# One decoder block on one core: a planner that charges changes of partitions, score products on quarters of the array, and a norm weight made from a column

## The chip, the core and the metric

The kernel runs on one core of one Trainium2 chip. The metric is device time in microseconds (us) of one execution. A core has a matrix engine (PE, with its weight loads shown as PEld), a vector engine (DVE), a scalar engine (ACT), GpSimd (POOL), and SyncE (SP), from which all loads and stores of this kernel are issued to 16 DMA engines. PE writes to PSUM, eight banks of 128 partitions by 512 f32 values; DVE and ACT read it from there.

## What is computed

One decoder block over 512 tokens of width 1024. Two groups of heads run side by side: RWKV-7 (eight heads of 64, a recurrence over tokens) and sparse attention with three branches; then an output projection and a SwiGLU feed-forward part.

```python
y = rmsnorm(h, norm1_w) @ w_in                       # one projection for both groups
# RWKV-7, for each token t and head:
sa = einsum('bhij,bhj->bhi', S, -kk_t)
S  = S * w_t + sa[..., None] * (kk_t * a_t) + v_t[..., None] * k_t
o_t = einsum('bhij,bhj->bhi', S, r_t)
# attention: softmax(q k / 8) v over compressed, selected and window keys, gated and added
h = h + concat([o_rwkv, o_nsa]) @ w_out
h = h + (silu(n2(h) @ ffn_w1) * (n2(h) @ ffn_w3)) @ ffn_w2
out = rmsnorm(h, final_norm_w)
```

## The kernel before

The kernel is written as a list of operations in program order (class Kern), which a planner (class Program) sorts. `add` records each operation and `cost` gives it a duration in ns. `layout` links it to those that it must wait for, and `schedule` walks through time: at each step the engine that is free first takes the ready operation of the highest rank. A rank is the longest path to the end, plus `ahead`, a priority that `go(part)` sets from the table PRIO. The planner also picks DVE or ACT for a copy (`nc.copy`), and a PSUM bank for each product. Each engine then executes its list in that order, fixed when the kernel is built. SP's queue is ordered in the same way.

For PE the planner keeps the array shape of each operation (`mode`: rows and columns, 32, 64 or 128). A change of shape costs 100 ns (L497 and L498), and an operation of the last shape is preferred if its rank is at most STAY below the best (L457). Matmuls that use other columns of the array than the one before are glued to it (`glue`, L260 to L265): they are placed together and count 53 or 27 ns. Two generators are woven together: `merge` runs the recurrences as the main stream and takes work from `filler` (projections, compression, attention) by RATIO; `zip` runs one pair's recurrence with the next pair's preparation, by ZIP.

The stages by the profile's clock: first norm and the first projection (0 to 20 us), further projections and the preparation of the first of four head pairs (to about 100), recurrences of the four pairs beside the projections (to about 300), attention (about 265 to 359), the output projection (to 402), the feed-forward part (to 740).

What the change touches:

- `consts` and `norm1` (first norm). The weight of the norm is loaded as a row and broadcast by the DMA to all 128 partitions (`n1w`, 512 KB), second in SP's order. `norm_T` squares a tile of x, takes the reciprocal root, multiplies by the weight on DVE, and transposes on PE.
- `rw_prep` prepares one pair of heads (p = 0 to 3, two heads on 64 partitions each). BKB holds for head 0 the columns [kk | k2] and for head 1 [k2 | kk], written by four multiplications on 64 partitions. For each head and each half of the chunks (cg) four matmuls of 64 rows by 128 columns fill one PSUM bank with scores, and one DVE multiplication by a mask moves the bank to SC. Then comes the substitution (`subst`: 45 short DVE operations, then 32x32 products from L1245 on, `doubl`), and later transposes of BK, eight for each head, to one bank a head.
- `attention`. A unit is a pair of query heads and a branch (eight units). `probs` computes and normalises the weights P. For each block j of 128 keys, the blocks of P of both heads are transposed on PE and copied out of PSUM (PT), and two 128x64 matmuls with v add to the bank `po`; then the next j.

Of the kernel before, what the change touches and what calls it, by code (L numbers as in the profile page):

```python
# [176 lines left out]
class Op:  # L177
    __slots__ = ("i", "eng", "name", "args", "kw", "r", "w", "dur", "pred", "succ", "banks", "rank", "n", "est", "start", "tag", "alt", "cols", "glue", "ahead", "beside", "mode", "work")
# [10 lines left out]
class Program:  # L189
# [7 lines left out]
    def __init__(self, tc):  # L197
        self.tc, self.nc = tc, tc.nc
        self.ops, self.slots, self.free, self.regions = [], [], {}, {}
        self.table, self.pre, self.side = [], None, None  # L200
        self.ahead = 0
        for e in self.ENG:
            setattr(self, e, Proxy(self.add, e))
# [24 lines left out]
    def add(self, eng, name, args, kw):  # L228
# [16 lines left out]
        op.dur = self.cost(op)  # L245
        if name == "preload_act_table_set":
# [6 lines left out]
        if eng == "tensor":  # L253

            m, c0 = size(kw["lhsT"]) if name == "matmul" else 128, op.w[0].p0 // 32
# [3 lines left out]
            p = 2 if name == "transpose" else 1 if kw["rhs"].dtype == R32 else 4  # L259
            op.work = p * size(op.w[0]) * l.n * size(l) / 128 ** 2  # L260
            op.cols = set(range(c0, c0 + m // 32))
            if self.side and not op.cols & self.side:
                self.ops[-1].glue = op
                self.side = self.side | op.cols
# [19 lines left out]
    def cost(self, op):  # L284
# [26 lines left out]
    STAY = 3000  # L311

    def moved(self, op):

        return math.prod((op.w + op.r)[0].shape) * 4 / 360
# [75 lines left out]
    def schedule(self):  # L391
# [33 lines left out]
        order, last_pe = [], None  # L425
        while len(order) < len(self.ops):
# [17 lines left out]
            while ready[e] and not op:  # L444
# [4 lines left out]
                if o.alt:  # L449
# [5 lines left out]
                    op = o  # L455
                    break
                if pick and pick[0][0] + self.STAY < x[0]:  # L457
# [7 lines left out]
                if not new or have >= self.RESERVE[new[0].key] + len(new):  # L465
                    same = e != "tensor" or not last_pe or o.mode == last_pe.mode
# [26 lines left out]
            if e == "sync" and len(out) == 8:  # L493
                t = max(t, out.pop(0))
            if e == "tensor":

                if last_pe and last_pe.mode != op.mode:  # L497
                    t += 100  # L498
# [12 lines left out]
            if e == "sync":  # L511
                dma = max(t + 1100, dma) + self.moved(op)
                end = dma + 900
# [62 lines left out]
class Kern:  # L576
# [150 lines left out]
    def consts(self):  # L727
        nc, a = self.nc, self.a
        self.cc = Split([(0, self.tl(self.cst, [128, 256], "cc")), (256, None)])
# [1218 lines left out]
```

## Time and profile before

| what | us |
|---|---|
| median of 3 runs (746.73 to 747.71) | 746.78 |
| the profiled execution | 746.66 |
| its span, first to last instruction | 744.8 |
| PE busy | 713.2 |
| DVE busy | 620.0 |
| ACT busy | 429.9 |

A line of the trace is L560 for nearly all instructions, since one loop issues them; rows are told apart by engine, operation and shape. A shape such as `64*128 64x128` is of a matmul on 64 rows and 128 columns of the array (rows*columns) that streams 128 values through each of the 64 rows. An ordinary f32 matmul is recorded as two instructions, a transpose or an fp32r matmul as one. Busy time is the union of the recorded intervals; ends of matmuls are modelled and run past the start of the next one.

### The profile page before, as it was taken

The page shows a single profiled execution, that of the slowest core. Times are in us where ns is not written, and L with a number is a line of the kernel's source. Part 1 is how long each engine was busy: PE and PEld are TensorE (multiplying, and loading weights), DVE is VectorE, ACT ScalarE, POOL GpSimd, SP SyncE. Part 2 cuts the span into 40 slices and gives each one's busy share as a digit, 9 for nine tenths or more (in the row PEclk, how much of TensorE's full clock was granted, in tenths as well). Part 3 has the DMA queues.
Part 4 walks back from the last instruction along what each step waited for, and adds up shares of the span by engine and source line. Part 5 has one row for each costly group of instructions (what it writes and reads, how often), then busy time and mean ns, then how long its engine had stood idle before and what let it go on. Part 6 is the DMA issues. An engine that isn't in the chain of part 4 may idle for free. (4 is left out here: it accounts for less than half of the span.)

```text
span 744.8 us, 14644 instructions
## 1 busy us (share of the span) xinstructions
PE 713.2 (96%) x5540; PEld 606.7 (81%) x5540; DVE 620.0 (83%) x1480; ACT 429.9 (58%) x948; POOL 3.7 (1%) x39
## 2 busy tenths in 40 slices
PE   5999999999989989999999999999999999999996
PEld 4988975768768666666788999999999999888785
DVE  6956988986997999798538999999999994687886
ACT  6555466554554688898336566565555552533545
POOL 0000000000000000000000000000000000000000
PEclk9999999999999999999999999999999999999999
DMA  8222326202110010533311233333333307464453
GB/s 318 72 77 62 98 78 199 75 27 74 41 31 28 16 45 1 170 103 96 114 57 71 72 114 114 114 120 108 114 100 114 101 22 258 159 216 149 139 171 116
DMA packets 39829, 77.37 MB, mean 104 GB/s; under 512 B 4432, under 2 KB 8912, under 8 KB 39760
## 3 DMA queue, kind: packets, MB, share of 16 engines
q1 hardware_dynamic: 39760, 76.45, 31.5%
q8 instruction: 43, 0.70, 0.4%
q14 instruction: 26, 0.21, 0.1%
HBM read 72.24 MB, written 4.19 MB: 103 GB/s over the span
## 5 line engine op out<-in xcount | busy, mean ns | idle before, releaser
L560 PE MATMUL ps<-s,s 128*128 128x256 f32 (+11 forms) x5412 | 710.4, 304 | 25.2 <-DVE s L560 19.1
L560 PEld LDWEIGHTS ps<-s,s 128*128 128x128 f32 (+5 forms) x5412 | 604.0, 170 | 130.2 <-DVE s L560 37.9
L560 DVE TENSOR_TENSOR s<-s,s 128x512 fp32r<-128x512 f32 (+18 forms) x662 | 378.4, 607 | 38.0 <-ACT s L560 18.9
L560 ACT ACTIVATE s<-s 128x512 fp32r<-128x512 f32 (+9 forms) x395 | 237.3, 619 | 226.7 <-DVE s L560 87.0
L560 ACT ACTIVATE s<-ps 128x256 f32<-128x256 f32 (+9 forms) x286 | 103.4, 376 | 43.2 <-PE ps L560 39.7
L560 DVE TENSOR_TENSOR s<-ps,s 128x256 f32<-128x256 f32 (+5 forms) x174 | 86.2, 506 | 29.7 <-PE ps L560 28.5
L560 ACT ACTIVATE s<-s,s 128x512 f32<-128x512 f32 (+4 forms) x142 | 72.1, 526 | 26.3 <-DVE s L560 25.0
L560 DVE COPY s<-ps 128x256 f32<-128x256 f32 (+6 forms) x77 | 32.4, 429 | 6.7 <-PE ps L560 5.4
L560 DVE CUSTOM_DVE_ANT_0 s<-ps,s 128x384 f32<-128x384 f32 (+3 forms) x64 | 29.8, 484 | 3.9 <-PE ps L560 3.7
L560 DVE SCALAR_TENSOR_TENSOR s<-s,s,s 128x512 f32<-128x512 f32 (+2 forms) x32 | 19.4, 630 | 13.8 <-DMA s<-in_n1w 6.6
L560 ACT ACTIVATE s<-ps,s 128x512 f32<-128x512 f32 (+1 forms) x34 | 20.1, 621 | 12.8 <-PE ps L560 12.6
L560 DVE SCALAR_TENSOR_TENSOR s<-ps,s,s 64x64 f32<-64x64 f32 (+1 forms) x62 | 23.9, 385 | 4.1 <-PE ps L560 1.5
L560 DVE CAST s<-s 128x512 fp32r<-128x512 f32 (+6 forms) x27 | 10.9, 409 | 14.5 <-PE ps L560 10.4
L560 DVE TENSOR_SCALAR s<-s,s 128x128 f32<-128x128 f32 (+4 forms) x67 | 21.4, 353 | 1.4 <-ACT s L560 0.8
L560 DVE STREAM_SHUFFLE s<-s 128x8 f32<-128x8 f32 (+14 forms) x60 | 14.0, 234 | 0.1
L560 ACT ACTIVATION_READ_ACCUMULATOR s<-s,s 128x1 f32 x64 | 12.1, 190 | 0.0
L560 DVE SCALAR_TENSOR_TENSOR s<-s,s 128x128 f32<-128x128 f32 (+1 forms) x26 | 8.9, 347 | 0.4
L560 ACT ACT_TABLE_LOAD x6 | 7.7, 1283 | 0.8 <-PEq L1935 0.7
L560 DVE TENSOR_TENSOR_SCAN s<-s,s 128x512 f32<-128x512 f32 x4 | 4.9, 1219 | 1.9 <-ACT s L560 1.9
L560 DVE COPY s<-s 64x512 f32<-64x512 f32 (+3 forms) x16 | 5.2, 323 | 0.8 <-PE ps L560 0.5
L560 DVE CAST s<-ps 128x512 fp32r<-128x512 f32 x7 | 4.8, 682 | 0.6 <-PE ps L560 0.6
L560 DVE DVE_READ_ACCUMULATOR2_ANT s<- 128x1 f32 x64 | 5.2, 82 | 0.0
(19 smaller groups left out, 41.2 us busy)
## 6 DMA issues: line engine op xcount, KB each, us to landing
s<-in_ffn_w SPq DMA_DIRECT2D x90, 256.0 KB, 2.7
s<-in_ffn_w SPq DMA_DIRECT2D x34, 512.0 KB, 3.8
s<-in_w_in_r SPq DMA_DIRECT2D x28, 256.0 KB, 2.7
s<-in_x SPq DMA_DIRECT2D x8, 512.0 KB, 5.4
s<-in_cw SPq DMA_DIRECT2D x16, 256.0 KB, 3.3
s<-in_w_out SPq DMA_DIRECT2D x8, 512.0 KB, 3.5
s<-in_w_in_n SPq DMA_DIRECT2D x8, 256.0 KB, 2.7
scr<-s SPq DMA_DIRECT2D x4, 512.0 KB, 2.6
```

The source lines that it names most:

```text
L560: ins = f(*[real(x) for x in op.args], **{k: real(x) for k, x in op.kw.items()})
```

## The change

- Planner: the array cells that a matmul uses are now pairs of row and column strips. A matmul is glued to those before it if it shares no cell with them, and no column strip in the same bank. DVE and ACT operations get a mode too, first partition and number of partitions, and a change is charged 110 ns. `keep` glues consecutive PE operations without condition. Latencies and DMA costs are changed (TOPE 80 instead of 120 towards PE, 80 more after f32 products, 300 instead of 360 bytes per ns), the scan costs 1140.
- Parameters: STAY is 500 for PE and 0 for the others; RATIO, ZIP and several priorities change.
- `rw_prep`: BKB is [kk | k2] for both heads, by two multiplications on 128 partitions. Each score matmul becomes two of 64x64, one for each output half; the four of a chunk lie on the four quarters of the array. The transposes of BK become products with the identity, in the same arrangement.
- `attention`: all transposes of a unit come first, then its eight matmuls with v, glued.
- `norm1`: the weight arrives as eight columns behind the first 256 columns of constants. Each half is copied to 128 columns a block by broadcast, transposed on PE, and copied out of PSUM.

```diff
@@ add
+        op.mode = (op.w[0].p0, op.w[0].n) if eng in ("vector", "scalar") and op.w else None
...
-            op.cols = set(range(c0, c0 + m // 32))
-            if self.side and not op.cols & self.side:
+            op.slow = p == 4
+            op.cols = {(r, c) for r in range(l.p0 // 32, l.p0 // 32 + op.mode[0] // 32) for c in range(c0, c0 + m // 32)}
+            bank, at = op.w[0].buf, {c for _, c in op.cols}
+            if self.side and not any(op.cols & q or at & {c for _, c in q} and b is bank for q, b in self.side):
                 self.ops[-1].glue = op
...
             else:
-                self.side = op.cols
+                if self.keep and self.ops and self.ops[-1].eng == "tensor":
+                    self.ops[-1].glue = op
+                self.side = [(op.cols, bank)]
@@ cost, lat, schedule
+        if op.name == "tensor_tensor_scan":
+            return 1140
...
-    STAY = 3000
+    TOPE = 80
+    STAY2 = 0
+    DRAIN = {"tensor": 100, "vector": 110, "scalar": 110, "gpsimd": 0, "sync": 0}
+    STAY = 500
...
-            t = self.LAT[p.eng] + (120 if op.eng == "tensor" else 0)
+            t = self.LAT[p.eng] + (self.TOPE if op.eng == "tensor" else 80 if p.eng == "tensor" and p.slow else 0)
...
-                if pick and pick[0][0] + self.STAY < x[0]:
+                if pick and pick[0][0] + (self.STAY if e == "tensor" else self.STAY2) < x[0]:
...
-                    same = e != "tensor" or not last_pe or o.mode == last_pe.mode
+                    same = last[e] in (None, o.mode)
...
+            if last[e] not in (None, op.mode):
+                t += self.DRAIN[e]
+            last[e] = op.mode
@@ norm1
-        wd = nc.sync.dma_start(out=w, in_=a["n1w"][None, :].to_broadcast([128, D]))
         wb = [w[:, :512], w[:, 512:]]
+        for n in range(2):
+            b = self.tl(self.p1, [128, 512], "nb", bufs=2)
+            nc.copy(b.rearrange("p (k m) -> p k m", k=4), self.nwc[:, 4 * n:4 * n + 4, None].to_broadcast([128, 4, 128]))
+            pt = self.ps("r")
+            for k in range(4):
+                self.tr(pt[:, k * 128:(k + 1) * 128], b[:, k * 128:(k + 1) * 128], self.ident)
+            nc.copy(wb[n], pt)
@@ Kern
-    RATIO = 0.684
+    RATIO = 0.787
-    PRIO = {'score': 18000, 'gn': -10000, 'wout': -5000, 'prep': -11000, 'wout_load': -8000, 'rope_tables': 13000, 'cmp_probs': 41000, 'nsa0': 12000, 'compress': 3000, 'subst': 21000, 'inproj': -4000, 'probs': 1000, 'attention': 2000, 'loras': 20000, 'norm1': 2000, 'out': -10000, 'doubl': 8000}
-    ZIP = 1.099
+    PRIO = {'score': 54000, 'gn': 10000, 'wout': -3000, 'prep': -15000, 'wout_load': -8000, 'rope_tables': 25000, 'cmp_probs': 41000, 'nsa0': 12000, 'compress': 3000, 'subst': 29000, 'inproj': -4000, 'probs': 1000, 'attention': 2000, 'loras': 20000, 'norm1': 2000, 'out': -6000, 'doubl': 28000, 'nsa_in': 8000}
+    ZIP = 1.239
@@ rw_prep
-        BK = [BKB[HS[h]] for h in range(2)]
+        BK = [[BKB[HS[h], :, HS[x ^ h]] for x in range(2)] for h in range(2)]
...
-        for h in range(2):
-            for x, t in ((h, kk), (1 - h, k2)):
-                nv.tensor_tensor(BKB[HS[h], :, HS[x]], c3(t)[HS[h]], c3(ip)[HS[h]], op=A.mult)
+        for x, t in enumerate((kk, k2)):
+            nv.tensor_tensor(BKB[:, :, HS[x]], c3(t), c3(ip), op=A.mult)
...
-        for h in range(2):
-            for cg in range(2):
-                pt = self.ps("r").rearrange("p (c x n) -> p c x n", x=2, n=64)
-                for c in range(4):
-                    self.mm(pt[:, c], BK[h][:, cg * 4 + c], KR[HS[h], cg * 4 + c])
-                nv.tensor_tensor(SC[:, cg * 4:cg * 4 + 4, :, CS[h]], pt, msk, op=A.mult)
-                yield
+        for cg in range(2):
+            pts = [self.ps("r").rearrange("p (c x n) -> p c x n", x=2, n=64) for h in range(2)]
+            for c in range(4):
+                for h in range(2):
+                    for x in range(2):
+                        self.mm(pts[h][HS[x], c], BK[h][x][:, cg * 4 + c], KR[HS[h], cg * 4 + c])
+            for h in range(2):
+                nv.tensor_tensor(SC[:, cg * 4:cg * 4 + 4, :, CS[h]], pts[h], msk, op=A.mult)
+            yield
...
-            for c in range(8):
-                self.tr(pt[:, c], BK[h][:, c], self.ident[HS[h], HS[h]])
+        for c in range(8):
+            for h in range(2):
+                for x in range(2):
+                    self.mm(pts[h][HS[x], c], BK[h][x][:, c], self.ident[HS[h], HS[h]])
@@ attention
+                PT = []
                 for j in range(NT):
                     n = 512 - 128 * j
-                    v = self.vW[:, j, br * 128 + g * 64:br * 128 + g * 64 + 64]
-                    PT = []
...
+                for j in range(NT):
+                    v = self.vW[:, j, br * 128 + g * 64:br * 128 + g * 64 + 64]
                     for x in range(2):
-                        self.mm(po[self.HS[x], 128 * j:], v, PT[x], br == 0 and j == 0, False)
-                    yield
+                        self.mm(po[self.HS[x], 128 * j:], v, PT[2 * j + x], br == 0 and j == 0, False)
+                        self.nc.keep = True
+                self.nc.keep = False
+                yield
```

## Rows read from the trace of the kernel before

**Rows 1.** The page: span, PE's busy us (share) and instructions, granted clock in tenths.

```profile
span 744.8 us, 14644 instructions
...
PE 713.2 (96%) x5540; PEld 606.7 (81%) x5540; DVE 620.0 (83%) x1480; ACT 429.9 (58%) x948; POOL 3.7 (1%) x39
...
PEclk9999999999999999999999999999999999999999
```

**Rows 2.** Sums by stretch: length, busy us (instructions) of each engine, clock, DMA, GB/s.

```profile
0.00:20.00 20.00, 11.37 (x54) 9.48 (x55) 13.26 (x30) 14.35 (x30) 0.57 (x8) 1.00 0.81 296
...
100.00:300.00 200.00, 186.86 (x2102) 141.92 (x2101) 174.96 (x594) 125.05 (x331) 2.05 (x18) 1.00 0.18 55
300.00:360.00 60.00, 59.29 (x401) 37.88 (x399) 51.37 (x159) 48.30 (x131) 0.00 (x0) 1.00 0.35 115
...
402.00:620.00 218.00, 215.96 (x1791) 214.88 (x1790) 208.67 (x369) 133.95 (x263) 0.00 (x0) 1.00 0.32 101
```

**Rows 3.** Waits of PE, 100 to 300 us: total us, times, longest us.

```profile
PE ps L560 <- DVE s L560: 9.2, 15, 1.6
```

**Rows 4.** Timeline, 210 to 224 us: start us, us, instructions merged [idle before <-releaser].

```profile
214.13 3.83 PE L560 MATMUL ps<-s,s 32*32 32x32 f32 x140 [1.57 <-DVE s L560]
...
217.27 1.37 DVE L560 TENSOR_TENSOR s<-s,s 64x512 f32<-64x512 f32 x2
...
219.17 2.43 PE L560 MATMUL ps<-s,s 32*32 32x32 f32 x42 [1.21 <-DVE s L560]
```

**Rows 5.** PE by form, whole span: xcount | busy us, mean ns | idle before.

```profile
L560 PE MATMUL ps<-s,s 64*128 64x128 f32 x128 | 16.2, 282 | 0.3 <-DVE s L560 0.2
...
L560 PE MATMUL ps<-s,s 64*64 64x64 f32 x240 | 9.1, 222 | 0.0
...
L560 PE MATMUL ps<-s,s 128*64 128x512 f32 x32 | 8.5, 611 | 0.0
...
L560 PE MATMUL ps<-s,s 64*128 64x64 f32 x64 | 3.1, 230 | 0.0
L560 PE MATMUL ps<-s,s 128*32 128x512 f32 x16 | 2.1, 604 | 0.2 <-ACT s L560 0.2
```

**Rows 6.** PE by form, 74.5 to 78.5 us, then 183.56 to 184.55 us.

```profile
L560 PE MATMUL ps<-s,s 64*128 64x128 f32 x31 | 4.0, 279 | 0.0
...
L560 PE MATMUL ps<-s,s 64*128 64x128 f32 x16 | 1.2, 285 | 0.0
```

**Rows 7.** DVE by form, whole span.

```profile
L560 DVE TENSOR_TENSOR s<-ps,s 128x512 f32<-128x512 f32 x54 | 35.9, 684 | 21.9 <-PE ps L560 21.7
...
L560 DVE TENSOR_TENSOR s<-s,s 64x512 f32<-64x512 f32 x16 | 10.8, 680 | 0.2
```

**Rows 8.** PE by form, 308.7 to 310.6 us.

```profile
L560 PE MATMUL ps<-s,s 128*64 128x512 f32 x4 | 1.0, 594 | 0.0
L560 PE MATMUL ps<-s,s 128*64 128x384 f32 x4 | 0.8, 486 | 0.0
L560 PE MATMUL ps<-s,s 128*64 128x256 f32 x4 | 0.6, 379 | 0.0
L560 PE MATMUL ps<-s,s 128*64 128x128 f32 x2 | 0.3, 273 | 0.0
```

**Rows 9.** Timeline, 0 to 26 us.

```profile
4.33 1.06 ACT L560 ACTIVATE s<-s 128x1024 f32<-128x1024 f32 x1 [2.31 <-DMA s<-in_x]
...
6.57 1.42 DVE L560 SCALAR_TENSOR_TENSOR s<-s,s,s 128x512 f32<-128x512 f32 x2 [6.57 <-DMA s<-in_n1w]
...
7.38 7.47 PE L560 MATMUL ps<-s,s 128*128 128x128 f32 x32 [7.38 <-DVE s L560]
...
8.85 1.13 ACT L560 ACTIVATE s<-ps 128x512 fp32r<-128x512 f32 x2
...
16.55 0.53 ACT L560 ACTIVATE s<-s 128x408 fp32r<-128x408 f32 x1
...
17.14 9.12 PE L560 MATMUL ps<-s,s 128*128 128x408 f32 x53 [0.87 <-ACT s L560]
```

More of the change, by code (lines that the diff above doesn't have):

```diff
@@ L177 @@
 class Op:
-    __slots__ = ("i", "eng", "name", "args", "kw", "r", "w", "dur", "pred", "succ", "banks", "rank", "n", "est", "start", "tag", "alt", "cols", "glue", "ahead", "beside", "mode", "work")
+    __slots__ = ("i", "eng", "name", "args", "kw", "r", "w", "dur", "pred", "succ", "banks", "rank", "n", "est", "start", "tag", "alt", "cols", "glue", "ahead", "beside", "mode", "work", "slow")
 class Proxy:
@@ L199, in __init__ @@
         self.ops, self.slots, self.free, self.regions = [], [], {}, {}
-        self.table, self.pre, self.side = [], None, None
+        self.table, self.pre, self.side, self.keep = [], None, None, False
         self.ahead = 0
@@ L253, in add @@
         if eng == "tensor":
-            m, c0 = size(kw["lhsT"]) if name == "matmul" else 128, op.w[0].p0 // 32
+            m, c0 = size(kw["lhsT"] if name == "matmul" else args[1]), op.w[0].p0 // 32
             l = kw["lhsT"] if name == "matmul" else args[1]
@@ L424, in schedule @@
                 offer(op)
-        order, last_pe = [], None
+        order, last_pe, last = [], None, dict.fromkeys(self.ENG)
         while len(order) < len(self.ops):
@@ L511, in schedule @@
             if e == "sync":
-                dma = max(t + 1100, dma) + self.moved(op)
-                end = dma + 900
+                dma = max(t + 900, dma) + self.moved(op)
+                end = dma + 850
                 out.append(end)
@@ L733, in consts @@
         self.cc.parts[1] = 256, self.tl(self.cst, [128, NCST - 256], "cc1")
-        self.order = [nc.sync.dma_start(out=self.cc[:, 0:256], in_=a["cst"][:, :256])]
+        self.order = [nc.sync.dma_start(out=first, in_=a["cst"][:, :264])]
         nc.sync.dma_start(out=self.vec, in_=a["vecs"])
-        nc.sync.dma_start(out=self.cc[:, 256:], in_=a["cst"][:, 256:])
+        nc.sync.dma_start(out=self.cc[:, 256:], in_=a["cst"][:, 264:])
         nc.sync.dma_start(out=self.lev, in_=a["lev"])
@@ L802, in norm1 @@
             self.order.insert(i, nc.sync.dma_start(out=xs[i], in_=a["x"][i * 128:(i + 1) * 128, :]))
-        self.order.insert(1, wd)
         for i in range(NT):
@@ L898, in nsa_in @@
             dmas = [w[2] for w in W]
-            x, rest = self.order[:1] + self.order[2:5], self.order[1:2] + self.order[5:]
-            for n, op in enumerate(x[:1] + rest[:2] + dmas[:3] + x[1:2] + dmas[3:5] + x[2:3] + dmas[5:7] + x[3:] + dmas[7:] + rest[2:]):
+            x, cst = self.order[:4], self.order[4:]
+            for n, op in enumerate(x[:1] + cst + dmas[:3] + x[1:2] + dmas[3:5] + x[2:3] + dmas[5:7] + x[3:] + dmas[7:]):
                 op.ahead = 1e6 - 1e4 * n
@@ L1273, in rw_prep @@
         s["BK"] = BKs = self.tl(p1, [128, 8, 128], "BKs")
+        pts = [self.ps("r").rearrange("p (c n) -> p c n", n=64) for h in range(2)]
+        for c in range(8):
+            for h in range(2):
+                for x in range(2):
+                    self.mm(pts[h][HS[x], c], BK[h][x][:, c], self.ident[HS[h], HS[h]])
         for h in range(2):
-            pt = self.ps("r").rearrange("p (c n) -> p c n", n=64)
-            for c in range(8):
-                self.tr(pt[:, c], BK[h][:, c], self.ident[HS[h], HS[h]])
-            self.nc.copy(BKs[:, :, CS[h]], pt)
+            self.nc.copy(BKs[:, :, CS[h]], pts[h])
         yield
```

16 lines of the change are left out of this document (7 added, 9 removed).

## The prediction

> **What bounds the kernel now.** I read the page first. PE is busy 713.2 of 744.8 us, and the granted clock is at its full level, 2.4 GHz, in every slice [rows 1]. That makes PE work the currency of this kernel, but a busy PE is an average over stages, so the second view is the sums by stage [rows 2]. From 402 to 620 us (the FFN's first half) PE is idle 2 of 218 us and DVE 9; no line of that part is edited. From 300 to 360 us (attention) PE is idle 0.7 of 60 us. From 100 to 300 us, where the four head pairs' recurrences run beside the projections and the start of attention, PE is idle 13.1 of 200 us, and in the first 20 us it is idle 8.6. So PE work taken out before 402 us is worth its full length wherever something else is ready to run, and the two stretches with idle time are where an order can win or lose.
>
> The third view says who ends that idle time: from 100 to 300 us, 9.2 us in 15 waits end with DVE [rows 3]. The fourth shows one such place [rows 4]: PE stands 1.57 us before the 32x32 products of one pair and then 1.21 us more. Between these two waits DVE does other work, among it two multiplications on 64 partitions that write the tile BKB of the next pair (1.37 us); the chain of small products waits behind them in DVE's queue. The span ends 1.86 us short of the profiled execution's 746.66 us, and that execution is 0.12 us below the median of 746.78; I make the sum on 746.66 and add 0.12 at the end.
>
> **Scores.** Before, a score matmul has 64 rows of the array and all 128 columns, sixteen for each pair and 64 in all; each is recorded as two instructions, so 128 instructions, 16.2 us [rows 5], 0.253 us for one matmul. In the first pair they run one after the other: 31 records in 4.0 us, 0.26 us for one matmul [rows 6]. After, there are 128 matmuls of 64x64, and the planner glues four of them, one for each quarter of the array, into a set. What does a set cost? The trace has no set on four quarters, but it has both halves of the idea. Rows of the array: in the third pair the two heads' matmuls happen to alternate, and 16 records take 1.2 us where 16 of the first pair take 2.1 [rows 6]; two matmuls on different rows cost little more than one. Columns: four 128x32 matmuls of 512 columns take 2.1/2 = 1.05 us a set, and two 128x64 ones 8.5/8 = 1.06 us [rows 5]; a set costs what one matmul costs, however many share the columns. So 32 sets at 0.26 us = 8.3 us, a saving of 7.9 us. The best case is half of 16.2, a saving of 8.1.
>
> Each bank still has to be emptied by a mask multiplication on DVE, 0.684 us at 128x512 [rows 7], 16 of them, 10.9 us, which neither version changes. Before, a pair's scores kept PE 4.2 us and DVE 2.7, and PE was the later; after, PE needs 2.1 and DVE is the later. If PE finds nothing else to do meanwhile, the scores cost 10.9 us and the saving is 16.2 - 10.9 = 5.3. PE's idle share in this stretch is 7% [rows 2], so other work is mostly at hand; I take 7.9 and keep 5.3 as the end. The Trainium skill speaks against the change here: its page TensorEngine Tiling (Array Packing), section Performance Considerations, says that tiling speeds up TensorE but not the emptying of PSUM, which can become the bound. By that sentence the term would be 5.3 and the sum 2.6 us smaller; the rows show DVE at 87% of this stretch, near to it but not there.
>
> **The transposes of BK.** Sixty-four transposes of 64x128 (3.1 us [rows 5]) become 128 ordinary f32 products with the identity, again in 32 sets of four. The nearest row is the 64x64 products of 64 columns: 240 records, 60 sets of two, 9.1 us, 0.152 us a set [rows 5]. 32 x 0.152 = 4.9 us, so +1.8 us. If the sets are as cheap as the transposes were, 0. I take 1.8, since that row has the same size and type.
>
> **DVE in the preparation.** The sixteen multiplications on 64 partitions that write BKB (10.8 us, 0.680 us each [rows 7]) become eight on 128 partitions. A 64x512 operation takes what a 128x512 one takes, 0.68 us, so 8 x 0.68 = 5.4 us of DVE work goes. On PE that is worth nothing where PE is full; it is worth something in the 9.2 us of waits that DVE ends [rows 3], since these multiplications stand in front of the small products that PE waits for [rows 4].
>
> **Attention.** For each of eight units (a pair of heads and a branch) the weighted sums over v, four pairs of 128x64 matmuls, stood each behind its own transposes; now all eight transposed blocks come first and the eight matmuls follow glued together. No arithmetic changes. What is saved is PE's change between a whole-array shape and a half one. The planner prices a change at 0.1 us (L497 and L498). Thirty-two blocks becoming eight would save 24 entries and 24 exits, 4.8 us. But in before some pairs already stand together: at 308.7 to 310.6 us all four sizes of a unit are there with no other product among them [rows 8]. So 0 to 4.8; I take half, 2.4 us. What is added is a wait: the first of the eight matmuls now waits for the last of eight PSUM copies, and PE then runs about 2.3 us in which it feeds neither DVE nor ACT. PE's cover is the next unit's score products; with PE idle only 0.7 of 60 us there, I cost this at nothing, and it is among what would show as PE idle after 300 us if the cover is thin.
>
> **Start.** The broadcast load of the norm's weight (512 KB) goes, with its issue on SP's queue ahead of everything but the first x tile. In its place the first constants load carries eight more columns, and two broadcast copies, eight transposes and two copies out of PSUM make the same tile. In the trace ACT starts on x at 4.33 us, as soon as it lands, and DVE on the weight at 6.57 [rows 9]. Without the 512 KB all that is behind it lands 2.2 us earlier by the gap between the landings, or 1.8 us by the stretch's mean rate of 296 GB/s [rows 2]. Against that, the first norm multiplication now waits for a chain: constants at about 4.8 (their 132 KB at that rate behind x), a copy of 0.6 and a hop, the four transposes with their hop as between 7.38 and 8.85 in the trace, 1.5 [rows 9], another copy of 0.6: about 7.5, where before it was 6.57, 0.9 us later. DVE and ACT are idle or waiting then, so the added copies cost only this. PE becomes full at 17.14, released by ACT's split of a weight tile at 16.55 [rows 9]. Following the transfers this moves 1.8 to 2.2 earlier, following the first norm 0.9 later; I take 1.0 us of gain, between.
>
> **The order.** The planner gets other constants: DVE and ACT are charged 110 ns when an operation's partitions differ from the last one's, the latencies towards PE change, PE's preference for staying in one shape (STAY) falls from 3000 to 500, RATIO and ZIP and the priorities change: score 18000 to 54000, doubl 8000 to 28000, subst 21000 to 29000. The last three pull the pairs' preparation ahead of the projections. All engines execute in the order fixed at build, so this can move PE's idle time either way. No row of before shows the new order. Together with the eight DVE operations I take 2 us out of the 13.1, with bounds of 6 less and 6 more.
>
> **Sum.** -7.9 + 1.8 - 2.4 - 1.0 - 2.0 = -11.5; 746.66 - 11.5 + 0.12 = 735.3 us.
>
> **Rivals.** (a) DVE becomes the later one in 100 to 300 us: the scores save 5.3, the shorter preparation and the order save nothing. 735.3 + 2.6 + 2.0 = 739.9. For it: DVE 87% busy in that stretch and the waits that it ends; against it: 5.4 us of its own work goes. This is the case of the skill's sentence on emptying PSUM. (b) The idle time shrinks by 5.6 instead of 2, and the start follows the transfers with 2.2: 735.3 - 3.6 - 1.2 = 730.5. For it: the waits stand at exactly the small products whose priority rises. (c) Slower: the products of the substitution. Their 32x32 stage waits on a row of dozens of short DVE operations. If subst and doubl are placed in PE's order before DVE can have finished them, PE stands, and nothing behind it may pass. One pair lost 1.57 + 1.21 = 2.8 us so [rows 4]. The gain of 11.5 is eaten, and 1.5 us more, when each of the four pairs loses 3.3 us more than now: 748.3 us. Below 2.9 more for a pair it isn't slower than before. Against it: the planner charges DVE more than before, and so will rather expect it late. (d) The quarters don't run four at a time but two: 64 sets of scores at 0.26 = 16.6 (+0.4), 64 of BK at 0.152 = 9.7 (+6.6): +0.4 + 6.6 - 2.4 - 1.0 - 2.0 = +1.6, 748.4 us. Rows and columns each overlap in the trace, so this is unlikely.
>
> **Chances and range.** About 0.2% (1.5 us) is what a measurement of this kernel can tell from no change. Forecast, 731 to 739: 0.54. (a), 739 to 745: 0.20. (b): 0.12. No measurable change, with scores at 5.3, attention at 0, the start at +0.9 and the order losing 3: 0.05. (c): 0.07. (d): 0.02. Faster 0.86, same 0.05, slower 0.09. The range leaves out the far half of (b), and all that is slower than (a): 729 to 744.5.
>
> **What would show it.** The by-form rows of PE: 256 records of 64x64 with 128 columns at about 8.3 us of busy time; near 10.9 with PE idle beside them (a) holds, near 16 (d). The 64x64 products of 64 columns at 9.1 + 4.9 us. No 64x512 multiplication of SBUF tiles left on DVE except the splits. PE idle between 100 and 300 us at 11, under 8 for (b), over 24 for (c). PE full by 16 us. The four sizes of 128x64 products together in every unit. I am wrong in the sum's main term if the score records shrink as told and the idle time grows by as much.

## The result, and the profile after

The changed kernel takes 739.79 us (739.35 to 742.02), beside 747.25 us for the kernel before on the same chip: a ratio of 0.9898, 95% interval 0.9864 to 0.9932, so 7.5 us or 1.0% faster. The forecast was 735.3, its range 729 to 744.5. The sign and the range held, but the time lies above the forecast's own band of 731 to 739, in the band of rival (a), 739 to 745. A third of the expected gain of 11.5 us is missing, and the sections below look for it.

The page of the kernel after (span; busy us, share and instructions of each engine), which answers to [rows 1] (L570 is here the line that was L560):

```profile
span 737.5 us, 15291 instructions
...
PE 705.3 (96%) x5868; PEld 604.1 (82%) x5868; DVE 620.2 (84%) x1476; ACT 425.6 (58%) x948; POOL 3.7 (1%) x39
```

The span fell by 7.3 us, from 744.8 to 737.5. PE's busy time fell by 7.9, from 713.2 to 705.3. So PE's idle time, span less busy, went from 31.6 to 32.2 us: it didn't shrink by the 3 us that the start and the order were to bring (1.0 + 2.0), it grew by 0.6. The sums by stage, which answer to [rows 2] (one stage, 20 to 100 us, is new):

```profile
0.00:20.00 20.00, 13.70 (x67) 12.02 (x68) 14.46 (x34) 13.25 (x30) 0.57 (x8) 1.00 0.78 283
20.00:100.00 80.00, 77.59 (x519) 66.45 (x518) 63.70 (x188) 42.15 (x85) 1.09 (x13) 1.00 0.24 71
100.00:300.00 200.00, 188.12 (x2390) 144.93 (x2390) 180.28 (x614) 129.63 (x353) 2.05 (x18) 0.99 0.19 57
300.00:360.00 60.00, 57.29 (x385) 39.15 (x382) 44.80 (x130) 43.25 (x115) 0.00 (x0) 1.00 0.40 123
402.00:620.00 218.00, 216.43 (x1774) 214.43 (x1772) 204.69 (x362) 127.75 (x250) 0.00 (x0) 1.00 0.34 110
```

PE's idle time in a stage is its length less the first busy number. It went from 8.6 to 6.3 us in the first stage, from 13.1 to 11.9 in the third, but from 0.7 to 2.7 in attention (300 to 360 us), and it is 2.4 us from 20 to 100 us, where the kernel before was idle 0.5. What was won in two stages was lost in two others: attention, which I had costed at nothing, and 20 to 100 us, which I had not costed.

PE's forms, which answer to [rows 5]: the scores, then the 64x64 products of 64 columns, with those of BK among them.

```profile
L570 PE MATMUL ps<-s,s 64*64 64x64 f32 x496 | 14.4, 226 | 0.0
...
L570 PE MATMUL ps<-s,s 64*64 64x128 f32 x256 | 8.8, 274 | 2.1 <-DVE s L570 2.1
```

The scores take 8.8 us where they took 16.2, so 7.4 saved (7.9 predicted). The small products take 14.4 where both forms took 9.1 + 3.1 before, so 2.2 added (1.8 predicted). Those are the change's main terms, and they came almost as told. Waits of PE from 100 to 300 us, which answers to [rows 3]:

```profile
PE ps L570 <- DVE s L570: 9.8, 17, 1.3
```

The waits on DVE are 9.8 us, where they were 9.2, although 5.4 us of multiplications on 64 partitions left DVE's preparation. DVE didn't get less to do: it is busy 620.2 us in all, as before (620.0), and 180.28 us from 100 to 300 us, where it was 174.96. Over the whole span 13 more copies that change the type (CAST, from SBUF to SBUF) run on DVE, 5.7 us more; the lines of before and after:

```profile
L560 DVE CAST s<-s 128x512 fp32r<-128x512 f32 (+6 forms) x27 | 10.9, 409 | 14.5 <-PE ps L560 10.4
L570 DVE CAST s<-s 128x512 fp32r<-128x512 f32 (+6 forms) x40 | 16.6, 418 | 8.3 <-PE ps L570 7.7
```

### The profile page after: what moved, and what is told of

It reads as the page before. It is cut to its first block, busy times and chain, and to the rows that moved or that the text cites. A ratio compares the mean times of both kernels' runs of the same rounds, so it can differ in the third digit from the quotient of the medians.

```text
span 737.5 us, 15291 instructions
## 1 busy us (share of the span) xinstructions
PE 705.3 (96%) x5868; PEld 604.1 (82%) x5868; DVE 620.2 (84%) x1476; ACT 425.6 (58%) x948; POOL 3.7 (1%) x39
## 4 chain that ended last, share of the span: by engine, by line
PE 59%; DVE 16%; ACT 3%; DMA 2%; issue 2%; DVEq 0%; ACTq 0%
PE ps L570 59%; DVE s L570 16%; ACT s L570 3%; DMA s<-in_w_out 1%; DMA s<-in_ffn_w 1%; DMA s<-in_w_in_r 0%; DVEq L570 0%; ACTq L570 0%
## 5 line engine op out<-in xcount | busy, mean ns | idle before, releaser
L570 PE MATMUL ps<-s,s 128*128 128x256 f32 (+8 forms) x5740 | 702.8, 300 | 26.1 <-DVE s L570 21.3
L570 PEld LDWEIGHTS ps<-s,s 128*128 128x128 f32 (+3 forms) x5740 | 601.7, 168 | 126.2 <-DVE s L570 35.9
L570 DVE TENSOR_TENSOR s<-s,s 128x512 fp32r<-128x512 f32 (+17 forms) x654 | 374.0, 609 | 40.9 <-ACT s L570 20.7
L570 ACT ACTIVATE s<-s 128x512 fp32r<-128x512 f32 (+8 forms) x385 | 231.0, 619 | 215.2 <-DVE s L570 90.3
L570 ACT ACTIVATE s<-ps 128x256 f32<-128x256 f32 (+9 forms) x293 | 105.8, 381 | 53.3 <-PE ps L570 48.1
L570 DVE TENSOR_TENSOR s<-ps,s 128x256 f32<-128x256 f32 (+5 forms) x174 | 86.7, 508 | 22.2 <-PE ps L570 20.7
L570 ACT ACTIVATE s<-s,s 128x128 f32<-128x128 f32 (+4 forms) x144 | 72.4, 519 | 26.1 <-DVE s L570 24.0
L570 DVE COPY s<-ps 128x256 f32<-128x256 f32 (+7 forms) x75 | 31.9, 432 | 12.3 <-PE ps L570 11.6
L570 DVE CUSTOM_DVE_ANT_0 s<-ps,s 128x128 f32<-128x128 f32 (+3 forms) x64 | 29.6, 484 | 3.4 <-PE ps L570 3.0
L570 DVE SCALAR_TENSOR_TENSOR s<-ps,s,s 64x64 f32<-64x64 f32 (+1 forms) x62 | 24.0, 387 | 7.1 <-PE ps L570 4.1
L570 ACT ACTIVATE s<-ps,s 128x512 f32<-128x512 f32 (+1 forms) x35 | 20.3, 602 | 12.6 <-PE ps L570 12.3
L570 DVE SCALAR_TENSOR_TENSOR s<-s,s,s 128x512 f32<-128x512 f32 (+2 forms) x32 | 19.4, 630 | 7.0 <-DMA s<-in_n2w 5.0
L570 DVE CAST s<-s 128x512 fp32r<-128x512 f32 (+6 forms) x40 | 16.6, 418 | 8.3 <-PE ps L570 7.7
L570 DVE TENSOR_SCALAR s<-s,s 128x128 f32<-128x128 f32 (+4 forms) x65 | 21.1, 364 | 1.2 <-ACT s L570 0.7
L570 DVE STREAM_SHUFFLE s<-s 128x8 f32<-128x8 f32 (+14 forms) x60 | 14.1, 236 | 0.1
L570 ACT ACTIVATION_READ_ACCUMULATOR s<-s,s 128x1 f32 x64 | 12.2, 191 | 0.0
L570 DVE COPY s<-s 32x256 f32<-32x256 f32 (+5 forms) x15 | 4.9, 329 | 5.7 <-DMA s<-in_cst 4.8
L570 DVE SCALAR_TENSOR_TENSOR s<-s,s 128x128 f32<-128x128 f32 (+1 forms) x26 | 9.0, 349 | 0.3
L570 DVE TENSOR_TENSOR_SCAN s<-s,s 128x512 f32<-128x512 f32 x4 | 4.9, 1220 | 1.9 <-ACT s L570 1.9
L570 DVE DVE_READ_ACCUMULATOR2_ANT s<- 128x1 f32 x64 | 5.3, 83 | 0.0
L570 DVE TENSOR_SCALAR s<-s 128x128 f32<-128x128 f32 (+4 forms) x24 | 4.7, 210 | 0.3
```

What stands on the lines that cost most here:

```text
L570: ins = f(*[real(x) for x in op.args], **{k: real(x) for k, x in op.kw.items()})
```

## The experiments

Each kernel is the one after, or the one before where that is said, with the edit shown. Ratios are to the kernel before on the same chip, with the 95% interval. Whatever is edited, the planner lays out the whole order anew, and it can differ anywhere; so an experiment on one part asks two things at once, what the part is worth and what the new order is worth. The four kernels at the end, each with its order fitted again, are there to part the two.

### The operations alone, and the order alone

All edited operations, under the planner, RATIO, ZIP and PRIO of before:

```diff
-    DRAIN = {"tensor": 100, "vector": 110, "scalar": 110, ...}
-    STAY = 500
+    STAY = 3000
...
-    RATIO = 0.787
+    RATIO = 0.684
...
```

> All edits of the operations (scores and BK on quarters, attention, norm weight from a column), sorted by the planner, constants and priorities of before. Theory W (the gain is PE work taken out; idle time is much the same under either order): the score records stay near 8.8 us, BK's near 5, PE busy near 706, time 739 to 742. Theory O (the order carries the gain, or spoils it): PE busy as under W, but idle time in 20 to 360 us over 20 us, time 744 or more.

756.12 us, ratio 1.0119 (1.0104 to 1.0135): the same operations that the change brings are 8.9 us slower than the kernel before when the order isn't made for them. The row of 100 to 300 us:

```profile
100.00:300.00 200.00, 181.38 (x2271) 137.78 (x2272) 164.35 (x547) 115.28 (x298) 2.08 (x18) 0.97 0.19 56
```

PE is idle 18.6 us there instead of 13.1, and the granted clock is 0.97 of full on average. DVE is busy 164.35 us where it was 174.96: it isn't overloaded, it is waited for. The expectation missed one thing: PE's busy time is 718.3 us and not near 706. The lower clock is a part of that, and the scores another: their records take 12.3 us and not 8.8, since the old planner doesn't glue the four quarters. So the planner's edit is needed for the work itself, and not only for the order.

The operations of before under the planner, RATIO, ZIP and PRIO of after (the edit is against the kernel after; one of its places is shown):

```diff
-        for x, t in enumerate((kk, k2)):
-            nv.tensor_tensor(BKB[:, :, HS[x]], c3(t), c3(ip), op=A.mult)
+        for h in range(2):
+            for x, t in ((h, kk), (1 - h, k2)):
+                nv.tensor_tensor(BKB[HS[h], :, HS[x]], c3(t)[HS[h]], c3(ip)[HS[h]], op=A.mult)
...
```

> The operations of before, sorted by the planner, constants and priorities of after. Theory W: PE busy within 2 us of 713, time 745 to 748. Theory O: the planner's new charges take idle time out by themselves: 742 or less; or, if its priorities cost idle time as seen after at 85, 92 and 321 us, 749 or more.

751.83 us, ratio 1.0049 (1.0029 to 1.0069). The new constants bring nothing by themselves either. The row of 100 to 300 us, of the fastest execution (748.56 us):

```profile
100.00:300.00 200.00, 186.98 (x2105) 144.63 (x2104) 173.22 (x590) 125.99 (x340) 2.30 (x18) 0.97 0.19 58
```

PE is idle 13.0 us there, as before, but the clock averages 0.97. Both halves of the change alone are slower than before, and together they are faster: the parts of this change don't add up, and a part's value has to be asked under an order that was fitted to it.

### The preparation of the recurrence

Only the new preparation (BKB on 128 partitions, scores and BK products on quarters), in the kernel before:

```diff
-        for h in range(2):
-            for x, t in ((h, kk), (1 - h, k2)):
-                nv.tensor_tensor(BKB[HS[h], :, HS[x]], c3(t)[HS[h]], c3(ip)[HS[h]], op=A.mult)
+        for x, t in enumerate((kk, k2)):
+            nv.tensor_tensor(BKB[:, :, HS[x]], c3(t), c3(ip), op=A.mult)
...
+                for h in range(2):
+                    for x in range(2):
+                        self.mm(pts[h][HS[x], c], BK[h][x][:, cg * 4 + c], KR[HS[h], cg * 4 + c])
```

> Before, with the preparation of a pair alone changed (BKB alike for both heads, scores and BK products on quarters). Theory W: scores 16.2 to about 8.8, BK products +2.2, so -5.2 us of PE work, and time 741 to 742.5. Rival D (DVE, which empties the score banks, is the later one there): -2 to -3, time 744 or more, with PE idle before and behind the score products.

756.12 us, ratio 1.0126 (1.0107 to 1.0144). Its score row, its sum and its waits of PE from 100 to 300 us:

```profile
L560 PE MATMUL ps<-s,s 64*64 64x128 f32 x256 | 12.3, 276 | 0.5 <-DVE s L560 0.5
```

```profile
100.00:300.00 200.00, 180.96 (x2306) 137.24 (x2307) 167.26 (x559) 119.78 (x314) 2.08 (x18) 1.00 0.19 56
```

```profile
PE ps L560 <- DVE s L560: 9.7, 14, 1.8
PE ps L560 <- ACT s L560: 6.2, 13, 1.1
PE ps L560 <- DMA s<-in_cw: 2.4, 3, 1.1
```

The old planner compares columns of the array only, so it doesn't glue the four quarters: the records take 12.3 us, not 8.8, and PE's busy time stays at 712.9 us (713.2 before). What makes the kernel slower is the idle time, 19.0 us in this stage, part of it now ended by ACT and by loads.

The kernel after with the old preparation:

```diff
-                self.mm(pts[h][HS[x], c], BK[h][x][:, c], self.ident[HS[h], HS[h]])
+                self.tr(pt[:, c], BK[h][:, c], self.ident[HS[h], HS[h]])
...
```

> After, with the preparation of a pair as before (scores 64x128, transposes of BK, four multiplications on 64 partitions). Theory W: 5.2 us more than after, 744.5 to 745.5. Rival D: only 2 to 3 us more, 742 to 743.

748.78 us, ratio 1.001 (0.9988 to 1.0033): 9.0 us slower than after, more than the whole gain. PE's busy time is 714.6 us, 9.3 more than after. The work that was put back explains only a part of that. By the rows before and after it is 5.2 (7.4 less 2.2); in this kernel itself the old scores take 13.4 us and not 16.2, and the 64x64 products and the transposes of BK 9.1 + 4.0, so it is 13.4 - 8.8 less 14.4 - 13.1, 3.3 us:

```profile
L570 PE MATMUL ps<-s,s 64*128 64x128 f32 x128 | 13.4, 282 | 1.5 <-DVE s L570 1.4
```

The idle time adds next to nothing: from 100 to 300 us it is 12.4 us, against 11.9. Most of the other 6 us is the clock's. Three rows of this kernel, 10 us each:

```profile
240.00:250.00 10.00, 6.65 (x151) 4.94 (x149) 9.83 (x41) 5.83 (x20) 0.00 (x0) 0.83 0.08 28
250.00:260.00 10.00, 10.00 (x121) 8.01 (x121) 5.47 (x16) 6.15 (x17) 0.00 (x0) 0.66 0.21 54
...
270.00:280.00 10.00, 8.61 (x40) 6.01 (x40) 9.62 (x38) 8.15 (x28) 0.00 (x0) 0.83 0.01 2
```

The granted clock averages 0.83, 0.66 and 0.83 of full there: part of the time it is at the lower of its two levels, 1.2 GHz. Between 241 and 248 us PE waited 0.65, 0.54, 1.31 and 0.83 us. PE is "busy" all of 250 to 260 us, and does less in it. What each row lacks of 1, times its 10 us, makes 6.8 us of full clock that these three lost; the kernel after lost 1.7 in its two such rows (last section).

### The priorities

The kernel after with RATIO, ZIP and PRIO of before, everything else kept:

```diff
-    RATIO = 0.787
+    RATIO = 0.684
-    PRIO = {'score': 54000, ... 'subst': 29000, ... 'doubl': 28000, ...}
-    ZIP = 1.239
+    PRIO = {'score': 18000, ... 'subst': 21000, ... 'doubl': 8000}
+    ZIP = 1.099
```

> After, with the priorities, RATIO and ZIP of before; operations and planner as after. Theory O (the values are fitted to one list of operations and one planner, and lose their worth with any other): slower than before, 750 to 756 us (the planner itself ends at 754.2 with them, and at 739.8 for after), all of it idle time of PE and DVE before 400 us. Theory W (PE work decides): PE work is that of after, 740 to 742.

755.81 us, ratio 1.0106 (1.0087 to 1.0126), 16.0 us slower than after with the same operations and the same planner. The page's PE row, and three rows of 10 us:

```profile
PE 716.6 (95%) x5868; PEld 612.8 (81%) x5868; DVE 622.4 (82%) x1480; ACT 422.7 (56%) x944; POOL 3.7 (0%) x39
```

```profile
190.00:200.00 10.00, 10.00 (x51) 8.17 (x50) 9.80 (x50) 4.20 (x13) 0.00 (x0) 1.00 0.16 53
200.00:210.00 10.00, 8.15 (x183) 6.72 (x182) 9.60 (x30) 5.94 (x15) 0.33 (x3) 0.71 0.14 32
...
280.00:290.00 10.00, 10.00 (x74) 7.35 (x76) 7.37 (x27) 7.68 (x24) 0.00 (x0) 0.69 0.01 2
```

PE's busy time is 716.6 us against 705.3 for the same 5868 instructions, because the clock averages 0.93 from 100 to 300 us; the rest is idle time (16.8 us in that stage, against 11.9). So an order costs twice: the waits themselves, and the slower clock after some of them.

### Attention

The weighted sums behind their own transposes again:

```diff
-                        self.mm(po[self.HS[x], 128 * j:], v, PT[2 * j + x], br == 0 and j == 0, False)
-                        self.nc.keep = True
-                self.nc.keep = False
-                yield
+                        self.mm(po[self.HS[x], 128 * j:], v, PT[x], br == 0 and j == 0, False)
+                    yield
```

> After, with attention as before (each j's two matmuls with v behind its transposes, none glued by force). Theory of the prediction: some 24 more changes of shape on PE, +2.4 us, 742. Theory O: the planner ends at 739.5 with it, 0.3 earlier than after: the glued block costs in waits what it saves in changes, 739 to 740.5, with PE's waits at 321 and 328 us smaller and more short ones.

743.31 us, ratio 0.9938 (0.9921 to 0.9954): 3.5 us slower than after. In the order of the trace PE changes its shape 150 times, where the kernel after has 114 changes, and PE's busy time is 708.7 us against 705.3: 36 changes and 3.4 us, about 0.1 us each. This is a division, not a measurement of one change, and rather low: from 100 to 300 us this kernel has the full clock, and the kernel after lost 1.7 us of it (last section). With these it would be 0.14.

The transposes first, as after, but the eight matmuls not glued:

```diff
-                        self.nc.keep = True
-                self.nc.keep = False
```

> After, with a unit's matmuls with v behind all its transposes but not glued. If the glue makes the waits of 1.0 and 0.6 us behind the blocks of 2.4 us in attention, PE idles less than after between 300 and 360 us, and the time is 1 us lower or the same; by the planner's own end it is 2.3 us higher, 742.

746.05 us, ratio 0.9973 (0.9964 to 0.9982): 6.3 us slower than after, with 152 changes, 38 more, and 4.1 us more of PE work; the rest is idle time, 7.9 us in the first stage (6.3 after) and 13.4 from 100 to 300 us (11.9 after). So under these priorities the glue is what makes the regrouping pay. What the regrouping costs under them shows in the sums of 300 to 360 us, first of attention_undone, then of keep_undone:

```profile
300.00:360.00 60.00, 58.77 (x383) 36.98 (x382) 51.93 (x155) 45.65 (x118) 0.00 (x0) 1.00 0.42 134
```

```profile
300.00:360.00 60.00, 57.34 (x368) 33.89 (x367) 51.09 (x148) 44.86 (x125) 0.00 (x0) 1.00 0.41 127
```

PE is idle 1.2 us with the old interleaving, and 2.7 with the transposes first, glued (after) or not. One place of it in the kernel after (timeline: start, us, merged instructions, idle before and releaser):

```profile
317.70 2.37 PE L570 MATMUL ps<-s,s 128*64 128x512 f32 x16
...
320.65 0.90 ACT L570 ACTIVATE s<-s,s 128x128 f32<-128x128 f32 x2
321.09 2.29 PE L570 MATMUL ps<-s,s 128*128 128x128 f32 x11 [1.02 <-ACT s L570]
```

PE runs the 16 instructions of one block for 2.37 us, and then stands 1.02 us for ACT.

### The first norm's weights

The broadcast load of 512 KB back in its place:

```diff
-            nc.copy(b.rearrange("p (k m) -> p k m", k=4), self.nwc[:, 4 * n:4 * n + 4, None].to_broadcast([128, 4, 128]))
...
+        wd = nc.sync.dma_start(out=w, in_=a["n1w"][None, :].to_broadcast([128, D]))
```

> After, with the first norm's weight as a broadcast load of 512 KB. Prediction: 1.0 us more than after, 740.5 to 741; the planner's own end says 1.65 more. If PE becomes full in after only 0.6 us earlier than in before (16.54 against 17.14), the start itself gives 0.6, and what is over comes from the order behind it.

740.24 us, ratio 0.9898 (0.9883 to 0.9912), the very ratio of the kernel after. The edit of the start is worth nothing that this measurement can tell, although PE is full only at 17.71 us without it, 1.2 us later than after.

### Orders fitted again

RATIO, ZIP and PRIO were found for each of the following kernels in the same way, by search on the planner's own end. First the kernel after, nothing else changed:

```diff
-    RATIO = 0.787
+    RATIO = 0.811
-    PRIO = {'score': 54000, 'gn': 10000, ... 'subst': 29000, ... 'doubl': 28000, ...}
-    ZIP = 1.239
+    PRIO = {'score': 38000, 'gn': 3000, ... 'subst': 15000, ... 'doubl': 34000, ...}
+    ZIP = 1.097
```

> After, with RATIO, ZIP and the priorities fitted once more by a search for the earliest end in the planner's own books; the operations are those of after. Theory O (the fit carries most): 735 to 738 us, with PE work as in after and the idle time before 400 us 3 to 5 us less. If the priorities of after are as good as the chip allows: 739 to 741.

735.84 us, ratio 0.9829 (0.9799 to 0.9859). The four executions took 733.98, 734.05, 737.62 and 737.92 us; the profile is of the third. The sums of two stages and the waits from 100 to 300 us:

```profile
100.00:300.00 200.00, 189.36 (x2395) 145.80 (x2394) 177.69 (x615) 132.07 (x357) 2.21 (x18) 0.98 0.19 56
300.00:360.00 60.00, 58.71 (x388) 41.29 (x387) 49.36 (x136) 42.28 (x112) 0.00 (x0) 1.00 0.43 141
```

```profile
PE ps L570 <- DVE s L570: 4.8, 10, 1.2
PE ps L570 <- ACT s L570: 3.6, 6, 1.5
```

```profile
L570 PE MATMUL ps<-s,s 64*64 64x128 f32 x256 | 8.6, 275 | 0.0
```

The waits on DVE are half of those after, but those on ACT grew from 1.2 to 3.6, so that PE's idle time in this stage falls only from 11.9 to 10.6 us. In attention PE is idle 1.3 us, although the transposes still come first, and from 20 to 100 us it is idle 0.4 us. The scores, the same sets of four, wait for nothing: the 2.1 us on DVE in their row after were the order's.

The operations of before under the new planner, whose edit isn't shown again, fitted in the same way:

```diff
-    RATIO = 0.684
+    RATIO = 0.799
-    PRIO = {'score': 18000, 'gn': -10000, ... 'subst': 21000, ... 'doubl': 8000}
-    ZIP = 1.099
+    PRIO = {'score': 61000, ... 'subst': 29000, ... 'doubl': 31000, ...}
+    ZIP = 0.903
```

> The operations of before under the planner of after, with RATIO, ZIP and priorities fitted by the same search. In the planner's books it ends 0.5 us before after_fit. Theory W (under orders fitted alike, PE work decides): some 8 us slower than after_fit (5.2 from scores and BK, 2 to 3 from attention), 744 to 746 us. Theory O (the operations are worth little, the fit all): within 2 us of after_fit, 735 to 740.

740.79 us, ratio 0.9909 (0.9878 to 0.994). The work of before, in an order that was merely fitted again, is as fast as the kernel after to 1.0 us. Equally fitted, the new operations are worth 740.79 - 735.84 = 5.0 us. That they are worth something is clear, since the executions don't overlap (738.94 to 744.65 here, 733.98 to 737.92 with the new operations); by the two intervals the size is known to some 3 us, and each side was fitted once. The profile here is of the slowest execution, 744.65 us, and has a stretch of lower clock:

```profile
20.00:100.00 80.00, 79.19 (x425) 69.83 (x423) 59.13 (x175) 40.48 (x82) 1.01 (x12) 0.94 0.22 67
```

The kernel after with the old preparation, fitted in the same way:

```diff
-    RATIO = 0.787
+    RATIO = 0.843
-    PRIO = {'score': 54000, ...}
-    ZIP = 1.239
+    PRIO = {'score': 37000, 'gn': 14000, ... 'subst': 20000, ... 'doubl': 28000, ...}
+    ZIP = 1.026
...
```

> After with the preparation of a pair as before, fitted by the same search. Theory W: 5.2 us slower than after_fit (7.4 of score work back, 2.2 of BK products gone), 741 to 743. Theory O: within 2 us of after_fit.

740.23 us, ratio 0.9897 (0.9874 to 0.992): the preparation is worth 4.4 us under fitted orders, where undoing it under the unfitted one cost 9.0. Its score row:

```profile
L570 PE MATMUL ps<-s,s 64*128 64x128 f32 x128 | 11.8, 283 | 1.2 <-DVE s L570 1.2
```

The old scores take 11.8 us here, not 16.2: many of their records now start in twos, some 5 ns apart, much as in the third pair [rows 6], where the two heads' matmuls happened to alternate (some 23 ns apart). So part of the edit's gain on the records was to be had from the order alone. Between the two fitted kernels the rows give 11.8 - 8.6 = 3.2 us for the scores less 13.7 - 12.7 = 1.0 for the products with BK among them, 2.2 us, half of the 4.4; the other half isn't shown by any row.

Last, one more planner line. It charges 53 ns for each further matmul of a set, 159 for the three that follow the first. The traces say otherwise: one 64x128 matmul of before took 0.253 us [rows 5], and a whole set of four takes 8.8/32 = 0.275, so the three further members cost some 22 ns together, 7 each. So the charge was lowered to 8 (and that for 32 columns from 27 to 14, which no row backs), and the order fitted again:

```diff
-                op.dur = 53 if m > 32 else 27
+                op.dur = 8 if m > 32 else 14
...
-    RATIO = 0.787
+    RATIO = 0.765
-    ZIP = 1.239
+    ZIP = 0.811
```

> The operations of after; one line of the planner changed, what it charges for a matmul that is glued beside another on other cells of the array: 8 and 14 ns instead of 53 and 27, since a set of four 64x64 score matmuls takes 0.218 us in the trace of after where the planner charges 0.377. Fitted by the same search. Theory: the planner sees PE free earlier than it does now and places less work in front of the chains that wait; time 1 to 4 us below after_fit, 732 to 735. Rival: the 53 ns were slack that covers what the planner doesn't know, and with less of it PE waits more: 736 to 740, with the idle time of PE before 400 us above after_fit's 20.4.

729.27 us, ratio 0.9731 (0.9694 to 0.9767), 2.7% faster than before, and better than the 732 to 735 that were expected; the medians on this chip are 18.8 us apart (748.03). The page and the stages are of the slowest of its seven executions, 733.13 us:

```profile
span 731.1 us, 15291 instructions
...
PE 703.5 (96%) x5868; PEld 605.1 (83%) x5868; DVE 616.9 (84%) x1471; ACT 426.6 (58%) x953; POOL 4.0 (1%) x39
```

```profile
20.00:100.00 80.00, 80.00 (x533) 69.42 (x532) 66.86 (x201) 44.05 (x88) 1.39 (x14) 1.00 0.25 75
100.00:300.00 200.00, 191.41 (x2492) 148.61 (x2490) 182.02 (x633) 137.29 (x378) 1.95 (x17) 1.00 0.22 67
300.00:360.00 60.00, 58.44 (x317) 41.12 (x314) 42.32 (x106) 33.91 (x91) 0.00 (x0) 1.00 0.34 111
```

PE's idle time is 27.6 us in all (731.1 - 703.5), the lowest of all kernels with these operations, the clock is full in these stages, and not one operation differs from the kernel after. How much of the 6.6 us between this kernel and the refitted one comes from the truer charge, and how much from a luckier end of the search, isn't told apart: each charge was fitted once, and 1 to 4 us were expected.

## Why the prediction was right, and where it was not

- **Scores: right.** 7.4 saved of 7.9. 32 sets at 8.8/32 = 0.275 us of busy time, where 0.26 was taken. That the quarters run only two at a time (rival d) fell with it, as 16 us would have stood in that row. The 16.2 of before was in part a matter of its order, though: under the new planner the same old scores take 13.4, 11.8 and 15.6 us (prep_undone, prep_old_fit, old_ops_fit).
- **BK products: right.** 2.2 added, 1.8 predicted; 1.5 in the refitted kernel (13.7 against 12.2).
- **DVE as the bound (rival a): its number, and half of its account.** It gave 739.9, and 739.79 was measured. One half of it came about: the shorter preparation and the order saved nothing, as PE's idle time grew by 0.6. The other half needs scores that save 5.3, and they save 7.4; that the number fits all the same is luck. The waits in the score row stand ahead of a pair's first set, and not between the sets, where a bank that DVE hasn't emptied would show (timeline of PE: start, us, merged instructions, idle before):

```profile
166.11 3.78 PE L570 MATMUL ps<-s,s 64*64 64x128 f32 x99 [0.88 <-DVE s L570]
...
215.36 4.82 PE L570 MATMUL ps<-s,s 64*64 64x128 f32 x80 [1.27 <-DVE s L570]
```

  In the refitted order they are gone, with DVE doing the same work. The Trainium skill's sentence on emptying PSUM (TensorEngine Tiling (Array Packing), Performance Considerations) is not what limits here: in the kernel after and in its two refits PE never waits between the sets of a pair. With the old planner it does once, for 0.5 us (score row of prep_on_before).
- **Attention: right in kind, too small in size, and with a cost that I put at nothing.** The regrouping is worth 3.5 us under the order after, not 2.4. The price of 0.1 us that the planner has for a change of shape is near what the two experiments give (3.4 us for 36, 4.1 for 38; up to 0.15 each if the clock's 1.7 us are booked to it). On this the Trainium skill agrees in kind (TensorEngine Tiling (Array Packing), Key Properties: changing the mode drains the engine) and has no number. The cover failed in this order: "PE's cover is the next unit's score products" is wrong by 1.5 us, the idle time that goes when the interleaving comes back. It is not the regrouping's own cost: the refitted order keeps the regrouping and is idle 1.3 us there. What attention is worth under fitted orders, no run shows.
- **Start: the step failed, at little cost.** PE is full at 16.54 us, 0.6 earlier than [rows 9] show, but the gain in time isn't there (norm_undone, the same ratio). The first norm multiplication now starts at 7.18 us, so my chain to 7.5 was a little long. PE's idle time in this stage falls by 2.3 us mostly because the eight added transposes fill 1.97 us of it:

```profile
5.29 1.97 PE L570 MATMUL ps<-s,s 128*128 128x128 f32 x8 [5.29 <-DVE s L570]
7.18 0.74 DVE L570 SCALAR_TENSOR_TENSOR s<-s,s,s 128x512 f32<-128x512 f32 x1
...
16.54 3.65 PE L570 MATMUL ps<-s,s 128*128 128x408 f32 x22 [0.24 <-DVE s L570]
```

- **Order and DVE: the step that failed.** I took 2 us out of 13.1 from 100 to 300 us, because eight multiplications leave DVE and the small products get a higher rank. DVE's time was filled with other work (among it the CAST lines above), and the waits went elsewhere: the 32x32 products of the substitution wait less for DVE, so (c) didn't come about, but the scores wait 2.1 us where they waited 0.3.

```profile
L560 PE MATMUL ps<-s,s 32*32 32x32 f32 x640 | 9.0, 194 | 4.1 <-DVE s L560 4.1
L570 PE MATMUL ps<-s,s 32*32 32x32 f32 x640 | 8.8, 193 | 2.8 <-DVE s L570 2.8
```

  In all 1.3 us went from that stage, but 1.9 came from 20 to 100 us, in two waits on DVE (1.17 us at 85.20, 0.95 at 91.79) that the refitted orders reduce to one of 0.34 or to none. My bounds of 6 either way held for this order, but were not wide enough for what an order can do: with the same operations and the same planner, the priorities, RATIO and ZIP alone move the time from 755.81 to 735.84, and the charge of a set with them to 729.27. What the prediction lacked is that one table of priorities reaches further than its rivals (b) and (c) lie apart.
- **The sum.** The span fell by 7.3 us, 4.2 less than the 11.5 of the forecast: 3.6 of that are idle time, 0.6 PE's work. 735.3 was the time of the work under an order as good as the one before was for its own. after_fit measures 735.84, but old_ops_fit shows that this reading is too kind: the order of before was itself 6.5 us from its refit, and with equal fits the change is worth 5.0 us. PE's work seems to fall as summed, by 8.6 us (714.2 to 705.6, 8.5 predicted), but both profiles have stretches of lower clock (0.94 from 20 to 100 us, 0.98 from 100 to 300 us), and that of the old operations the longer one (mean clock of the whole 0.991 against 0.994), so less than 8.6 is work. The idle time of the two profiles gives 2.0 back (28.2 to 30.2, where the forecast had it fall by 3). The 7.5 us measured are those 5.0, and 2.5 us net from an order that stands nearer to its refit (3.9 us away) than the one before did (6.5). The 6.5 are a refit together with the new planner; the old planner was not fitted again.
- **Left open.** PE's busy time fell by 7.9 us, though eight transposes (1.97) came in and 1.7 us of full clock were lost. Scores and BK give 5.2 of the 11.6 that this makes, 30 fewer changes of shape (144 to 114) 3 at 0.1 each and 4.5 at 0.15. The remaining 2 to 3.5 us lie spread over other forms, the largest being the 128x256 products (281.2 to 278.2 us); no run isolates them. Why the clock fell in one place and not in another is open too (last section).

## What to carry to other kernels

In a kernel whose order is fixed by a planner, an edit of the work has no value of its own: measure it with the order fitted again on both sides, or the fit's distance is booked to the edit (here 8.9 us slower, 7.5 faster and 5.0 faster are all "the same operations"). Before editing work, look whether the planner's charges are what the trace shows; one wrong charge, a set's further members at 53 ns, was corrected and refitted for 6.6 us, more than the edit was worth, though how much of that is the search's luck isn't told apart. Look at the clock of a profile before its busy time is read as work. And where a step regroups work "under cover", find the cover's own start in the timeline before putting its cost at nothing.

## What the runs showed of the hardware

The granted clock of TensorE can fall to its lower level inside a run of a kernel whose PE is 95% busy. In the kernel with the old priorities PE was busy all of 190 to 200 us, then waited 0.45 and 1.36 us, and the mean clock of 200 to 210 us was 0.71; with the old preparation it was 0.66 in 250 to 260 us. In the kernel after, two rows show it mildly:

```profile
250.00:260.00 10.00, 8.86 (x154) 6.30 (x150) 8.39 (x30) 6.40 (x22) 0.00 (x0) 0.91 0.07 28
260.00:270.00 10.00, 8.74 (x103) 7.06 (x100) 9.70 (x35) 9.09 (x24) 0.00 (x0) 0.92 0.11 29
```

The kernel before kept its full clock through waits of the same size (up to 1.08 us, where the kernel after has up to 1.07), with PE less busy than in these rows:

```profile
260.00:270.00 10.00, 8.47 (x202) 6.34 (x192) 9.66 (x35) 8.55 (x23) 0.00 (x0) 1.00 0.18 58
270.00:280.00 10.00, 8.08 (x52) 6.26 (x51) 8.68 (x35) 9.40 (x28) 0.00 (x0) 1.00 0.07 26
```

So the busy share of a row of 10 us doesn't tell by itself when the clock falls, and these runs don't settle what does. Its price is plain: 716.6 us of PE work instead of 705.3 for the same instructions, of which the 12 more changes of shape explain about 1.2. It also differs between executions of one kernel: old_ops_fit took 738.94 to 740.80 us at a mean clock of 0.999 and 744.65 at 0.991.
